# Attention's output projection of a two-layer diffusion trunk: first latents and context in one pass over the weights

## The chip, the cores and the metric

One core of a Trainium2 chip runs the whole program. The metric is the device time of one execution in microseconds (us), as the median over runs; lower is better.

## The reference

A trunk of two layers with D = 1024 works on 1024 latent tokens and 256 context tokens. Layer 0 mixes tokens by multi-head latent attention, layer 1 by bidirectional gated linear attention (GLA); each mixer is followed by an MLP with a squared ReLU. Around every mixer and MLP stand an RMS norm ahead and one behind, with shift, scale and gate per stream, and the residual sum. The part around the change, cut from the reference:

```python
y_lat = o_lat @ w_o            # latents, 1024 x 1024 by 1024 x 1024
y_ctx = o_ctx.reshape(B, C, MLA_HEADS * MLA_V) @ w_o      # context, 256 x 1024
...
def rms_norm(x, g):
    xf = x.astype(jnp.float32)
    y = xf * lax.rsqrt(jnp.mean(xf * xf, axis=-1, keepdims=True) + NORM_EPS)
    return (y * g.astype(jnp.float32)).astype(x.dtype)
def modulate(h, shift, scale):
    return h * (1.0 + scale) + shift
def sqrelu_mlp(h, w1, w2):
    return jnp.square(jax.nn.relu(h @ w1)) @ w2
```

Both streams go through the same `w_o`. Its result is normed and gated, added to x, normed and modulated again, and is then h, the operand of the MLP.

## The kernel before

Activations lie with the features on the 128 partitions (8 tiles of 128 features, index k) and the tokens along the free axis. The tokens fall into three blocks: block 0, the context (256 wide), block 1, the first latents (512), block 2, the second latents (512). A product in single precision is made of three fast ones: `split` cuts an operand into a high part (a cast on ACT, L202) and a low part (a subtraction, L199, on DVE here), and `mm3` issues three matmuls, high by high (L232), high by low (L233), low by high (L234).

The output projection runs block by block, in the order 1, 0, 2. `out_items` makes one pass: two halves of the output features; in each half four PSUM banks, one for each 128 features, add up over the eight k. For every k and half a weight tile of 128x512 (`mla_wo`) is loaded and split, so a pass loads 16 tiles. Behind each half the four banks are copied to SBUF (L808, DVE), squared (L296 or L299, ACT) and the squares added up (L300, DVE). There are eight PSUM banks in all, twelve buffers "w" for split weights (six tiles), twelve "stg" for loaded tiles, 56 "m" buffers 512 wide, 16 "c" buffers 256 wide, and four "s" buffers for rows of x.

What stands behind a block's pass is a generator, `residual_norm_steps`, put on a list `bg`. It loads four rows of x into the "s" buffers, makes the inverse root mean square (`rstd`: an all-ones matmul over the sum of squares, L307; then three ACT operations, L313 to L315; then three DVE operations, L316 to L318), scales the eight tiles (L856), adds x (L858; each add frees a buffer for one of the other four rows), stores the sum to `x_scr` (L864), adds up squares again, makes a second `rstd`, and writes h: for block 1 by a scaling on DVE (L876) and a bias on ACT (L877), for the context by L324, L326 and L327, which give the split operand at once. The loads of x keep their written order on SP.

`tick` pays steps out of that list: each weight tile of a pass gives a credit of its width x 0.005, that is 2.56 for a wide block's and 1.28 for the context's, and each yield of the generator costs a number from a table. Block 1's steps ask for 46.2 in all, the context's for 35.8. With an empty list the credit stays at zero. A pass of 16 tiles gives 41.0 for a wide block and 20.5 for the context. What is not paid out by then runs when somebody asks for it: `mlp` calls `ready(h[1])`, which runs the list until block 1's h is written, splits it, builds the first two groups of MLP products for block 1 (`up_first`, 24 wide matmuls each; each ends in a DVE add from PSUM, L885, ReLU and square on ACT, L964 and L965, and stores to `a_scr` and `hid`, L978 and L980), and only then calls `ready(h[0])`, which runs the context's steps, and builds the context's products (`up_first_ctx`). From the program so written a scheduler makes a fixed order for each engine when the kernel is built; SP issues all the transfers named here.

Of the kernel before, what the change touches and what calls it, by code (L numbers as in the profile page):

```python
# [11 lines left out]
F32R = mybir.dt.float32r  # L12
# [7 lines left out]
P = 128  # L20
D = 1024
KT = D // P
CTX = 256
# [12 lines left out]
BLK_ORDER = (1, 0, 2)  # L36
BLK = ((0, 256), (256, 512), (768, 512))
# [8 lines left out]
PLAN = {'sq': [(1, 5), (1, 7), (2, 3), (2, 7), (0, 4), (2, 4), (1, 4), (2, 1), (1, 1)],  # L46
 'xlo': [5, 7, 6, 0],
 'wlo': [7, 1, 6, 0],
# [58 lines left out]
class Trunk:  # L107
# [648 lines left out]
    def after_attention(self, stop):  # L756
        I = self.I
        self.bg, self.credit = [], 0.0
        h = {b: self.out_proj(0, b, "mla_wo", self.o_scr, 0, I["xT"]) for b in BLK_ORDER}
        self.nc.sync.dma_start(self.cl, self.c_scr)  # L760
        if stop == "wo0":
            self.drain()
            return
        h = self.mlp(0, h)
        if stop == "mlp0":
            self.drain()
            return
        h = self.gla(h)
        self.mlp(1, h)
        self.drain()  # L770
# [21 lines left out]
    def out_items(self, res, l, b, wname, src, off, xsrc):  # L792
        t0, w = BLK[b]
        acc = self.m(512)[:, :w]
        o, ys = [], []
        for half in range(2):
            pss = [self.ps(w) for _ in range(4)]
            for k in range(KT):
                if half == 0:
                    o.append(self.msplit(self.load(src[k, :, t0 - off:t0 - off + w]), w, self.nc.vector))  # L800
                ww = self.weight(self.I[wname][k * P:(k + 1) * P, half * 512:half * 512 + 512], self.nc.vector)
                for n in range(4):
                    self.mm3(pss[n], self.cols(ww, n * P), o[k], k == 0, k == KT - 1)
                self.tick(w * PLAN["tk"][0])
                yield
            for n in range(4):
                y = self.m(512)[:, :w]
                self.nc.vector.tensor_copy(y, pss[n])  # L808
                self.sumsq(acc, pss[n], half == 0 and n == 0, w)
                ys.append(y)  # L810
        self.bg.append(self.residual_norm_steps(res, l, b, ys, acc, xsrc, 2, (l, 4), (l, 3), b != 0))

    def out_half_items(self, part, acc, ys):

        c = slice(part * 256, part * 256 + 256)
        o = []
        for half in range(2):
            pss = [self.ps(256) for _ in range(4)]
            for k in range(KT):
                if half == 0 and k % 2 == 0:  # L820
                    raw = self.slot("stg", 512)
                    self.nc.sync.dma_start(raw.rearrange("p (k t) -> p k t", t=256),
                                           self.z_scr[k:k + 2, :, c].rearrange("k p t -> p k t"))
                    zs = self.msplit(raw, 512, self.nc.vector)
                    o += [self.cols(zs, 0, 256), self.cols(zs, 256, 256)]
                ww = self.weight(self.I["gla_wo"][k * P:(k + 1) * P, half * 512:half * 512 + 512], self.nc.vector)
                for n in range(4):
                    self.mm3(pss[n], self.cols(ww, n * P), o[k], k == 0, k == KT - 1)
                self.tick(PLAN["tk"][4])
                yield  # L830
            for n in range(4):
                if part == 0:
                    ys.append(self.m())
                y = ys[half * 4 + n][:, c]
                self.nc.vector.tensor_copy(y, pss[n])
                self.sumsq(acc[:, c], pss[n], half == 0 and n == 0, 256)
# [845 lines left out]
```

## Time and profile before

| | before |
|---|---|
| median of 3 runs | 2870.64 us (2866.56 to 2875.65) |
| profiled execution | 2861.42 us |
| its span, first to last instruction | 2859.6 us |
| mean granted TensorE clock | 0.984 |
| PE busy | 2736.4 us (96%) |
| DVE busy | 2283.3 us (80%) |
| ACT busy | 1594.9 us (56%) |
| DMA, mean over the span | 187 GB/s |

The three passes of the output projection lie between 698.9 and 819.7 us of the span: block 1 to 742.6, the context to 766.3, block 2 behind it. The first two groups of MLP products follow until 836.0, then the context's products. PE is the TensorE, DVE the VectorE, ACT the ScalarE, SP the engine that issues the transfers. In a row of time the bracket at the end gives how long the engine stood idle before it and which instruction ended that idle time. Matmuls overlap, so the distance between the starts of two is what one costs.

### The profile page before, as it was taken

Reading aid. Unit: us, or ns where it says so; the run is one execution under the profiler, and the core shown is the slowest. Engines: PE = TensorE matmul, PEld = TensorE weight load, DVE = VectorE, ACT = ScalarE, POOL = GpSimd, SP = SyncE. Lnnn points to the kernel's source line nnn. Section 1 sums busy time; section 2 is a strip of 40 time slices with the busy share of each in tenths; the row PEclk is TensorE's granted clock in tenths of the full one; section 3 lists DMA queues with packets and bytes.
Section 4 is the critical chain, followed back from the end, with each engine's and each line's share of the span. In section 5 each row is a group of like instructions: output and inputs, shape, how many; then the busy total and the mean of one; then the engine's idle time right before and its main releaser. Section 6 shows DMA issues by size and latency. Waiting matters only on the chain.

```text
span 2859.6 us, 44542 instructions
## 1 busy us (share of the span) xinstructions
PE 2736.4 (96%) x14774; PEld 2355.4 (82%) x14774; DVE 2283.3 (80%) x4377; ACT 1594.9 (56%) x3341; POOL 535.3 (19%) x390
## 2 busy tenths in 40 slices
PE   8999898999989999999999999999888999999998
PEld 6788787898779888888888888888787778888877
DVE  6898989987788887698868684466998999777676
ACT  4667666666566444444544456666655745555443
POOL 2554444522000000000000032565520000000000
PEclk9999999999999999999999999999899999999999
DMA  7121434323636675498735566776685667577455
GB/s 252 40 80 61 132 99 142 101 74 120 225 121 233 199 255 181 154 338 289 257 123 177 170 200 191 246 241 220 200 265 202 232 207 257 192 272 260 144 181 160
DMA packets 319528, 535.50 MB, mean 187 GB/s; under 512 B 33216, under 2 KB 96576, under 8 KB 319296
## 3 DMA queue, kind: packets, MB, share of 16 engines
q1 hardware_dynamic: 313472, 527.40, 55.8%
q10 hardware_dynamic: 5760, 5.25, 0.5%
q8 instruction: 116, 1.90, 0.3%
q14 instruction: 116, 0.95, 0.1%
q0 software_dynamic: 64, 0.00, 0.0%
HBM read 412.19 MB, written 120.32 MB: 186 GB/s over the span
## 4 chain that ended last, share of the span: by engine, by line
PE 74%; DVE 14%; DMA 4%; ACT 4%; issue 2%; POOL 1%; SPq 0%; ACTq 0%; DVEq 0%; POOLq 0%
PE ps L233 23%; PE ps L232 22%; PE ps L234 22%; DVE m L199 2%; DVE y L708 1%; PE ps L735 1%; DVE ada L251 1%; DVE w L199 1%; ACT m L202 1%; DVE m L722 1%; PE ps L703 1%; PE ps L704 1%; PE ps L705 1%; ACT m L710 1%; PE ps L707 1%
## 5 line engine op out<-in xcount | busy, mean ns | idle before, releaser
L233 PE MATMUL ps<-m,w 128*128 128x512 f32 (+1 forms) x2320 | 896.0, 388 | 14.2 <-DVE m L199 14.1
L232 PE MATMUL ps<-m,w 128*128 128x512 f32 (+1 forms) x2320 | 876.1, 388 | 19.6 <-ACT m L202 15.9
L234 PE MATMUL ps<-m,w 128*128 128x512 f32 (+1 forms) x2320 | 891.0, 387 | 0.3 <-DVE w L199 0.2
L232 PEld LDWEIGHTS ps<-m,w 128*128 128x128 f32 x2320 | 438.4, 190 | 110.7 <-ACT m L202 22.9
L233 PEld LDWEIGHTS ps<-m,w 128*128 128x128 f32 x2320 | 440.5, 190 | 105.4 <-DVE m L199 20.7
L234 PEld LDWEIGHTS ps<-m,w 128*128 128x128 f32 x2320 | 439.7, 190 | 88.8 <-DVE w L199 2.4
L202 ACT CAST w<-stg 128x512 fp32r<-128x512 f32 (+2 forms) x510 | 312.0, 616 | 309.0 <-PE ps L233 246.0
L199 DVE TENSOR_TENSOR w<-stg,w 128x512 fp32r<-128x512 f32 x412 | 297.9, 727 | 113.0 <-ACT w L202 97.7
L202 ACT CAST m<-stg 128x512 fp32r<-128x512 f32 x296 | 177.7, 625 | 138.3 <-DMA stg<-hid 121.6
L233 PE MATMUL ps<-m,m 128*128 128x256 f32 (+1 forms) x632 | 196.4, 311 | 7.6 <-DVE m L199 4.1
L199 DVE TENSOR_TENSOR m<-stg,m 128x512 fp32r<-128x512 f32 x256 | 172.0, 685 | 39.3 <-ACT m L202 38.2
L232 PE MATMUL ps<-m,m 128*128 128x256 f32 (+1 forms) x632 | 188.1, 314 | 15.0 <-DVE m L1530 8.1
L232 PE MATMUL ps<-c,w 128*128 128x256 f32 (+1 forms) x664 | 188.3, 287 | 10.8 <-ACT c L326 4.7
L234 PE MATMUL ps<-m,m 128*128 128x256 f32 (+1 forms) x632 | 192.9, 305 | 0.0
L233 PE MATMUL ps<-c,w 128*128 128x256 f32 (+1 forms) x664 | 186.4, 283 | 1.3 <-DVE c L431 1.3
L234 PE MATMUL ps<-c,w 128*128 128x256 f32 (+1 forms) x664 | 185.1, 283 | 0.0
L1296 POOL DMA_DIRECT2D m<-m x2 | 1.2, 598 | 913.8 <-PE ps L233 913.1
L199 POOL TENSOR_TENSOR w<-stg,w 128x512 fp32r<-128x512 f32 (+2 forms) x98 | 131.0, 1338 | 194.4 <-ACT w L202 155.5
L202 ACT CAST w<-m 128x512 fp32r<-128x512 f32 x128 | 79.2, 621 | 116.3 <-PE ps L233 115.9
L232 PEld LDWEIGHTS ps<-m,m 128*128 128x128 f32 x632 | 123.1, 196 | 24.4 <-DVE m L1530 8.7
L885 DVE TENSOR_TENSOR t<-ps,t 128x512 f32<-128x512 f32 x164 | 111.0, 684 | 39.4 <-PE ps L234 31.5
L964 ACT ACTIVATE t<-t 128x512 f32<-128x512 f32 x109 | 68.7, 631 | 131.2 <-DVE t L885 126.0
(300 smaller groups left out, 5878.3 us busy)
## 6 DMA issues: line engine op xcount, KB each, us to landing
stg<-in_mlp_w SPq DMA_DIRECT2D x256, 256.0 KB, 4.3
stg<-hid SPq DMA_DIRECT2D x227, 256.0 KB, 3.9
hid<-t SPq DMA_DIRECT2D x205, 256.0 KB, 3.4
stg<-in_w SPq DMA_DIRECT2D x182, 256.0 KB, 3.4
ada<-in_adaT SPq DMA_DIRECT2D x80, 512.0 KB, 3.7
stg<-in_adaT SPq DMA_DIRECT2D x112, 256.0 KB, 4.1
stg<-in_gla_wv SPq DMA_DIRECT2D x64, 256.0 KB, 3.9
stg<-in_mla_wo SPq DMA_DIRECT2D x48, 256.0 KB, 4.7
```

Source lines behind the costliest of these rows:

```text
L199: eng.tensor_tensor(out=out, in0=a, in1=bits(hi), op=ALU.subtract)
L202: self.nc.scalar.copy(hi, src)
L232: mm(ps, lhs[0], rhs[0], start=first, stop=False, skip_group_check=shared)
L233: mm(ps, lhs[0], rhs[1], start=False, stop=False, skip_group_check=shared)
L234: mm(ps, lhs[1], rhs[0], start=False, stop=last, skip_group_check=shared)
L251: pin(nc.vector.tensor_tensor_reduce(out=w, in0=w, in1=self.cs[:, s], scale=1.0, scalar=0.0, op0=ALU.mult, op1=ALU.add, accum_out=c))
L703: mm(ps, qh[:, qs], kh, start=True, stop=False)
L704: mm(ps, qh[:, qs], kl, start=False, stop=False)
L705: mm(ps, ql[:, qs], kh, start=False, stop=False)
L707: mm(ps, qr[:, qs], rl, start=False, stop=True)
L885: eng.tensor_tensor(out=out, in0=a, in1=b, op=op)
L964: self.nc.scalar.activation(c, c, AF.Relu)
```

## The change

Blocks 1 and 0 go through one pass, `out_two`: each weight tile is loaded and split once and serves 12 wide matmuls for block 1 and then 12 narrow ones for the context. Six PSUM banks add up at a time: four for block 1, and two for the context, with two groups of 256 columns in each. The context's operands lie in "m" buffers, 256 columns of them used. Block 2 keeps its pass of its own. The norm steps of blocks 1 and 0 are both put on the list behind the merged pass, block 1's first; the merged pass therefore ticks with an empty list. What follows (L849 before, L886 after, and on) is the same text, 37 lines further down; `out_items` moves by two lines.

```diff
--- before.py
+++ after.py
@@ -756,7 +756,9 @@
     def after_attention(self, stop):
         I = self.I
         self.bg, self.credit = [], 0.0
-        h = {b: self.out_proj(0, b, "mla_wo", self.o_scr, 0, I["xT"]) for b in BLK_ORDER}
+        h = {1: [], 0: []}
+        self.run(self.out_two(h))
+        h[2] = self.out_proj(0, 2, "mla_wo", self.o_scr, 0, I["xT"])
         self.nc.sync.dma_start(self.cl, self.c_scr)
         if stop == "wo0":
             self.drain()
@@ -809,6 +811,41 @@
                 self.sumsq(acc, pss[n], half == 0 and n == 0, w)
                 ys.append(y)
         self.bg.append(self.residual_norm_steps(res, l, b, ys, acc, xsrc, 2, (l, 4), (l, 3), b != 0))
+
+    def out_two(self, h):
+
+        V = self.nc.vector
+        acc = {b: self.m(512)[:, :BLK[b][1]] for b in (1, 0)}
+        o, ys = {1: [], 0: []}, {1: [], 0: []}
+        for half in range(2):
+            pss = [self.ps() for _ in range(4)]
+            psc = [self.ps() for _ in range(2)]
+            for k in range(KT):
+                if half == 0:
+                    for b in (1, 0):
+                        t0, w = BLK[b]
+                        hi, lo = self.slot("m", w, F32R), self.slot("m", w, F32R)
+                        self.split(self.load(self.o_scr[k, :, t0:t0 + w]), hi, lo, V)
+                        o[b].append((hi, lo))
+                ww = self.weight(self.I["mla_wo"][k * P:(k + 1) * P, half * 512:half * 512 + 512], V)
+                for n in range(4):
+                    self.mm3(pss[n], self.cols(ww, n * P), o[1][k], k == 0, k == KT - 1)
+                for n in range(4):
+
+                    self.mm3(psc[n // 2][:, (n % 2) * CTX:(n % 2) * CTX + CTX], self.cols(ww, n * P), o[0][k],
+                             k == 0 and n % 2 == 0, k == KT - 1, True)
+                self.tick(768 * PLAN["tk"][0])
+                yield
+            for b in (1, 0):
+                w = BLK[b][1]
+                for n in range(4):
+                    p = pss[n] if b else psc[n // 2][:, (n % 2) * CTX:(n % 2) * CTX + CTX]
+                    y = self.m(512)[:, :w]
+                    V.tensor_copy(y, p)
+                    self.sumsq(acc[b], p, half == 0 and n == 0, w)
+                    ys[b].append(y)
+        for b in (1, 0):
+            self.bg.append(self.residual_norm_steps(h[b], 0, b, ys[b], acc[b], self.I["xT"], 2, (0, 4), (0, 3), b != 0))
 
     def out_half_items(self, part, acc, ys):
```

Of transfers there are 2022 on SP before and 2006 after: 16 loads of weight tiles fewer. The number of matmuls is the same. Where steps move, engine by engine:

On SP, before, the context's last four loads of x and its first stores stand while block 2's pass runs (`in_w` are MLP weights, `in_xT` the rows of x, `x_scr` the residual sum):

```order
L212 DMA stg_10498<-in_w 128x512
L212 DMA s_9805<-in_xT 128x256
L864 DMA x_scr<-m_9184 128x256
L212 DMA s_9811<-in_xT 128x256
L864 DMA x_scr<-m_9187 128x256
L212 DMA s_9837<-in_xT 128x256
L864 DMA x_scr<-m_9192 128x256
L212 DMA s_9845<-in_xT 128x256
```

After, all eight loads of the context's x stand behind the stores of the first two groups of MLP products (L1015 and L1017 are L978 and L980 before, L901 is L864):

```order
L212 DMA stg_10466<-in_w 128x512
L212 DMA stg_10472<-in_w 128x512
L1015 DMA a_scr<-t_9786 128x512
L1015 DMA a_scr<-t_9832 128x512
L1017 DMA hid_97<-t_9787 128x512
L1017 DMA hid_97<-t_9833 128x512
L212 DMA s_9866<-in_xT 128x256
L212 DMA s_9868<-in_xT 128x256
L212 DMA s_9870<-in_xT 128x256
L212 DMA s_9872<-in_xT 128x256
L212 DMA s_9886<-in_xT 128x256
```

The context's loads thus moved behind four stores that wait for the results of the MLP's first products.

On PE, the two all-ones matmuls of the context's norm before (`ps_9661` is an accumulator of block 2's pass, `ps_10020` one of the MLP products, `ps_10095` the context's first MLP product):

```order
L234 MATMUL ps_9664<-m_9504,w_9742 128x512
L307 MATMUL ps_9757<-m_8970,ones 128x256
L232 MATMUL ps_9661<-m_9537,w_9768 128x512
...
L234 MATMUL ps_10020<-m_9942,w_10001 128x512
L307 MATMUL ps_10038<-m_9802,ones 128x256
L232 MATMUL ps_10095<-c_10049,w_9948 128x256
```

And after (`ps_9848` and `ps_9802` belong to the MLP products, `ps_9995` is the context's first MLP product):

```order
L232 MATMUL ps_9848<-m_9749,w_9828 128x512
L307 MATMUL ps_9874<-m_8588,ones 128x256
L233 MATMUL ps_9802<-m_9750,w_9782 128x512
...
L234 MATMUL ps_9848<-m_9770,w_9829 128x512
L307 MATMUL ps_9938<-m_9883,ones 128x256
L232 MATMUL ps_9995<-c_9949,w_9776 128x256
```

The first of the two moved from inside block 2's pass to inside the 48 MLP matmuls, 26 of which stand ahead of it; the second still stands directly ahead of the context's products. Block 1's second all-ones matmul moved as well: 48 matmuls of block 2's pass stood ahead of it before, 168 stand ahead of it now.

On DVE, before, the low parts of block 1's h (L199 from an "m" into an "m" buffer), operands of the MLP products, stand among the last adds of the context's x (L858) and of its squares (L300):

```order
L858 TENSOR_TENSOR m_9409<-m_9409,s_9837 128x256
L199 TENSOR_TENSOR m_9915<-m_9583,m_9914 128x512
L199 TENSOR_TENSOR m_9919<-m_9610,m_9918 128x512
L858 TENSOR_TENSOR m_9414<-m_9414,s_9845 128x256
L199 TENSOR_TENSOR m_9923<-m_9613,m_9922 128x512
L199 TENSOR_TENSOR m_9927<-m_9640,m_9926 128x512
L300 TENSOR_TENSOR m_9802<-m_9802,t_9848 128x256
L199 TENSOR_TENSOR m_9931<-m_9683,m_9930 128x512
```

After, the last of these low parts stand around the context's first norm (L316 to L318) and behind its eight scalings (L893 is L856 before, L913 is L876):

```order
L199 TENSOR_TENSOR m_9757<-m_9753,m_9756 128x512
L913 SCALAR_TENSOR_TENSOR m_9760<-m_9223,m_78,m_9618 128x512
L316 SCALAR_TENSOR_TENSOR m_8588<-m_8588,c_9876 128x256
L317 TENSOR_TENSOR m_8588<-m_8588,c_9876 128x256
L318 SCALAR_TENSOR_TENSOR c_9876<-m_8588,c_9876 128x256
...
L199 TENSOR_TENSOR m_9764<-m_9760,m_9763 128x512
L913 SCALAR_TENSOR_TENSOR m_9767<-m_9228,m_78,m_9618 128x512
L893 SCALAR_TENSOR_TENSOR m_8949<-m_8949,m_80,c_9876 128x256
...
L893 SCALAR_TENSOR_TENSOR m_9248<-m_9248,m_80,c_9876 128x256
L199 TENSOR_TENSOR m_9771<-m_9767,m_9770 128x512
L922 TENSOR_TENSOR t_9787<-ps_9802,t_9786 128x512
```

The last low part is thus made after the context's scalings, directly ahead of the adds that end the MLP products (L922, before L885).

## Rows read from the trace of the kernel before

**Rows 1.** The page: the chain that ended last, by engine.

```profile
PE 74%; DVE 14%; DMA 4%; ACT 4%; issue 2%; POOL 1%; SPq 0%; ACTq 0%; DVEq 0%; POOLq 0%
```

**Rows 2.** By stretch: us, each engine's busy us, PEclk, DMA share, GB/s.

```profile
698.90:742.40 43.50, 43.50 (x192) 36.00 (x193) 26.88 (x47) 21.36 (x40) 0.00 (x0) 1.00 0.79 267
...
766.30:776.90 10.60, 4.32 (x13) 3.07 (x13) 10.60 (x21) 5.49 (x11) 0.00 (x0) 0.68 0.83 278
...
819.60:836.60 17.00, 13.81 (x51) 10.36 (x50) 14.27 (x29) 10.53 (x21) 0.00 (x0) 0.90 0.47 149
...
841.30:1000.00 158.70, 158.70 (x871) 137.96 (x872) 140.95 (x242) 92.09 (x172) 0.00 (x0) 0.99 0.61 199
```

**Rows 3.** Groups by line, 698.9 to 766.3: busy us, mean ns, idle before.

```profile
L202 ACT CAST w<-stg 128x512 fp32r<-128x512 f32 x37 | 23.0, 621 | 20.4 <-PE ps L233 16.8 <-DMA stg<-in_mla_wo 2.9 <-ACT t L299 0.3
...
L199 DVE TENSOR_TENSOR w<-stg,w 128x512 fp32r<-128x512 f32 x33 | 22.6, 687 | 14.1 <-ACT w L202 9.6 <-PE ps L233 2.2 <-DMA stg<-in_mla_wo 2.0
```

**Rows 4.** PE in time, two block borders: start us, us, what, idle before.

```profile
742.37 0.39 PE L234 MATMUL ps<-m,w 128*128 128x512 f32 x1
742.60 0.28 PE L232 MATMUL ps<-c,w 128*128 128x256 f32 x1
742.71 0.28 PE L233 MATMUL ps<-c,w 128*128 128x256 f32 x1
...
768.90 1.27 PE L232 MATMUL ps<-m,w 128*128 128x512 f32 x4 [2.58 <-ACT m L202]
...
773.88 0.80 PE L233 MATMUL ps<-m,w 128*128 128x512 f32 x1 [3.70 <-DVE m L199]
...
774.90 0.63 PE L233 MATMUL ps<-m,w 128*128 128x512 f32 x1
775.32 0.63 PE L234 MATMUL ps<-m,w 128*128 128x512 f32 x1
```

**Rows 5.** PE in time: all-ones matmuls (L307) and waits behind block 2's pass.

```profile
785.55 0.67 PE L307 MATMUL ps<-m,ones 128*128 128x512 f32 x1
...
808.30 0.38 PE L307 MATMUL ps<-m,ones 128*128 128x256 f32 x1
...
820.81 0.50 PE L232 MATMUL ps<-m,w 128*128 128x512 f32 x1 [1.00 <-ACT m L202]
823.50 0.73 PE L232 MATMUL ps<-m,w 128*128 128x512 f32 x2 [2.19 <-ACT m L202]
...
836.03 0.60 PE L307 MATMUL ps<-m,ones 128*128 128x256 f32 x2
841.28 0.59 PE L232 MATMUL ps<-c,w 128*128 128x256 f32 x2 [4.65 <-ACT c L326]
```

**Rows 6.** DVE and ACT in time: durations of wide and narrow operations.

```profile
741.11 1.88 DVE L808 COPY m<-ps 128x512 f32<-128x512 f32 x3
...
789.18 0.68 DVE L316 SCALAR_TENSOR_TENSOR m<-m,m 128x512 f32<-128x512 f32 x1
...
813.17 3.26 DVE L856 SCALAR_TENSOR_TENSOR m<-m,m,c 128x256 f32<-128x256 f32 x8
...
837.03 0.62 ACT L964 ACTIVATE t<-t 128x512 f32<-128x512 f32 x1
...
838.81 0.42 DVE L316 SCALAR_TENSOR_TENSOR m<-m,c 128x256 f32<-128x256 f32 x1 [1.82 <-ACT c L315]
```

**Rows 7.** SP's queue in time: the context's x loads and their stores.

```profile
816.79 0.33 SPq L212 DMA_DIRECT2D s<-in_xT  x1
817.17 0.42 SPq L864 DMA_DIRECT2D x_scr<-m  x1
817.69 0.38 SPq L212 DMA_DIRECT2D s<-in_xT  x1
```

**Rows 8.** DMA issues, 810 to 830 us; landing of x loads, 780 to 830.

```profile
s<-in_xT SPq DMA_DIRECT2D x4, 128.0 KB, 2.7
...
DMA to landing us min/median/max: 2.1/2.9/4.5
```

## The prediction

> **What bounds the kernel now.** I read the chain that ended last first: PE holds 74% of it, DVE 14% [rows 1]. So a saving on another engine is worth something only where PE waits for it, and I looked for PE's waits in the stretch that the change rewrites. The table by stretch shows them [rows 2]. Block 1's pass, 698.9 to 742.4, has PE busy all through. At the start of block 2's pass PE works 4.32 of 10.60 us at a granted clock of 0.68, while DVE is busy for all 10.60. At 819.6 to 836.6, the first MLP products, it works 13.81 of 17.0; from 836.6 to 841.28 it stands still for the context's norm, with a wait of 4.65 [rows 5]. From 841.3 to 1000 it is busy for 158.70 of 158.70: behind 841.3 nothing can swallow a delay for a long way. The whole case is therefore one question: when does the context's first MLP matmul start, today 841.28?
>
> **The removed work is hidden.** The change drops 16 weight loads, 16 ACT casts and 16 DVE subtractions of 128x512. In the two passes that are merged, the cast costs 0.62 us and the subtraction 0.69, but both engines' idle time ahead of them ends with PE: 16.8 of the casts' 20.4 us of idle time, that is, they wait for PE to give back weight buffers [rows 3]. 16 x 0.62 = 9.9 us of ACT and 16 x 0.69 = 11.0 us of DVE lie beside PE's busy 43.5 us, and are worth nothing there. The number of matmuls does not change: a wide one follows the next at 0.23 us, a narrow one at 0.12 [rows 4], so the merged pass is 192 x 0.227 + 192 x 0.119 = 66.4 us of PE in either order. Its start may slip by 0.3 us, since two operands are split ahead of the second weight tile. The merged pass then ends at 698.9 + 0.3 + 66.4 = 765.6, with block 1's last matmul 12 narrow ones before, at 764.2 instead of 742.6.
>
> **Step 1, block 2's start: a gain.** Before, PE ran 11 matmuls there in the 10.6 us from 766.3 to 776.9, worth 11 x 0.227 = 2.5: 8.1 us lost, to two waits (2.58 and 3.70) and to the low clock behind them, 1.2 instead of 2.4 GHz (0.43 us a matmul in place of 0.23) [rows 2, 4]. DVE caused it, busy with block 1's first norm. After, that norm has not begun, but another wait comes: the all-ones matmul for block 1's sums stands 4 matmuls into block 2, at about 766.5, and the sums need four wide copies (0.63), three narrow ones (as a narrow scaling, 0.41), three wide adds (taken as copies) and a weight subtraction on DVE: 4 x 0.63 + 3 x 0.41 + 3 x 0.63 + 0.69 = 6.3 [rows 3, 6]. The first copies run while the last accumulators fill, 1.4 us ahead of 764.2; I take 764.2 + 5.1 = 769.3 for the sums. PE waits 2.9 us and loses 1 to 1.7 us to the clock: about 4 lost for 8.1, **a gain of 4**. Block 2 ends at 765.6 + 43.6 + 4.5 + 1.1 for its two all-ones matmuls = 814.8, against 819.6 now.
>
> **Step 2, block 1's second norm: the gain is lost.** The steps of the norms are paid out by ticks: 20.5 us from block 0's pass and 41 from block 2's before, 41 alone after, since the list is empty during the merged pass. Block 1 asks for 46.2. Its second all-ones matmul, at 785.55 now [rows 5], moves to 168 matmuls into block 2, about 808.5. From there its chain reaches DVE after 3.6 us (785.55 to 789.18) [rows 5, 6], at 812.1; four operations of 0.6 (three for the norm, one weight subtraction), four scalings of 0.68, block 2's four copies, a weight subtraction and the operand's own subtraction make 812.1 + 2.4 + 2.7 + 2.4 + 0.6 + 0.1 = 820.3 for the first operand of the MLP. PE waits 5.3 us at its start, where it now waits 1.00 and 2.19 [rows 5]. The last operand comes later still, because DVE's order puts the context's first norm ahead of it: three small operations and eight scalings (3.26 us for the eight). That norm's all-ones matmul stands 26 matmuls into the 48 of the MLP, at 828 in place of 808.30; its chain reaches DVE after 2.8 us (836.03 to 838.81), and 1.3 for the three operations, 0.6 and 0.7 for an operand between, 3.3 for the scalings and 0.6 for the last subtraction [rows 5, 6] bring the last operand at 837.2, and the 48 matmuls end at **837.7, where they end at 836.03 now**.
>
> **Step 3, the context's norm: the loss.** Today the context's eight rows of x are loaded and added inside block 2's pass and behind it: from 816.79 on they run on SP as load, store, load, store, a pair each 0.95 us [rows 7], and only the second all-ones matmul and its chain (836.03 to 841.28, 5.25 us) are left at the end of the MLP products [rows 5, 7]. After, SP's order has the four stores of the MLP's results ahead of these loads; SP works in order, so the loads go out when the second result is there. From 837.7: the DVE adds of both results to 839.1 (2 x 0.69), two wide ACT passes of 0.62 [rows 6] and the store: the first load at about 841.0, the fourth at 842.1. A load of 128 KB lands 2.7 us after issue (median of four; of seven loads around it the least 2.1 and the most 4.5) [rows 8]. The first add frees its buffer at 844.1, and the other four loads leave at 0.95 us a pair, the last at 847.0; it lands at 849.7, and add, square and add make 850.9. Then the chain of 5.25 us: **the context's matmul at 856.1 against 841.28, +14.8 us.** What is queued behind the waiting stores on SP (the eight loads, the stores of x, the next MLP weights) has one impatient reader, this norm. PE stands still from 837.7 to 856 but for the all-ones matmul, about 18 us for 4.65 now.
>
> The operands of the context lie in wider buffers (the 56-deep pool instead of the 16-deep one). The rows show no wait on either; I price that from 0 to +1 us and take 0. From 841.3 on PE has no idle time to give back [rows 2], so the 14.8 us stay.
>
> **The rivals.** (A) **Covered after all, faster.** In the place of step 3, SP could reach the loads early. If the first results of the MLP came out some 20 us sooner than I order them, the norm would again run under PE's products; then step 1's 4 us remain and the stall at 836 (4.65) goes: -8.7, 2861.9. It decides at a first load before about 824. Against it speaks that these stores depend on PE's last matmul, and that PE's own start waits for DVE. (B) **Half the price, same.** The loads of the second four are not held back by buffers, and land in 2.1 us; the norm is then bound by DVE alone: sixteen operations of 0.41 us, 6.6 us from 840. All-ones at about 842.5, context at 847.5: +6, within what can be told from no change only just. For it: with the loads of the MLP's weights held back, DMA is quiet there, and 2.1 has been seen [rows 8]; against: there are four buffers for eight loads. (C) **The order as I add it**, +14.8. (D) **The spare banks run out.** Six accumulators leave two banks free for the next group, four before. At the merged pass's middle and at its end PE must wait for a copy (0.63) and a square ahead of each further accumulator, and each accumulator is 3 x 0.227 = 0.68 us of PE: a small wait if DVE does nothing else, 0.69 for each weight subtraction in between, up to five: 3.4 us a boundary and 6.9 for both, on top of C: +22. The Trainium skill (Perfetto Trace Analysis, Matmul Optimizations) wants all 8 PSUM banks used so that independent work overlaps, and its section on matmuls there wants groups to rotate through banks so that evacuation runs under the next group; this change holds six in one group, so by that rule D would be the case. Here the row on DVE's copies (0.63, below the 0.68 of an accumulator) speaks against most of it. That the change does not do what it says is excluded by the order of the engines: SP has 16 instructions fewer, all loads of this weight.
>
> **How the numbers follow.** The profiled run took 2861.42 us, 9.2 below the median of 2870.64, and the runs spread over 9.1; I add the shift to the median. C: 2870.64 + 14.8 = 2885.4. A difference of about 0.3% (8.6 us) is what a measurement can tell from no change. Chances: C 0.65, D 0.13, B 0.16, A 0.06. A is faster; B gives 2876.6, the same; C and D (2893) are slower, but C with landings of 2.1 in both batches (-1.2), a median at the low end (-4) and a late norm cheaper by 2 would be 2878, so a little of it (0.03) is the same. Faster 0.06, same 0.19, slower 0.75. The range takes B's upper part and D: C with landings of 4.5 us in both batches is +3.6, with D +10.5; I take 2874 to 2896.
>
> **What would show it.** Right: PE idle for 15 to 19 us ahead of the context's first matmul at 853 to 859, with the context's first load issued only behind the second result's store; PE at block 2's start waiting once, about 3 us, for the sums; the MLP's 48 matmuls ending within 2 us of 836. Step 1 is wrong if block 2's pass ends later than 819.6; step 2 if its all-ones matmul comes before 800; step 3 if the context's loads are issued before 835. A PE wait for a DVE copy in the middle of the merged pass would be D. And the whole is wrong if idle time of PE behind 1000 shrinks by as much as it grew here.

## The result, and the profile after

The changed kernel takes **2897.77 us** (2897.67 to 2901.66, 4 runs) against 2868.6 (2865.0 to 2875.65, 4 runs): ratio 1.0103, interval 1.0089 to 1.0117. It is slower by 29.2 us, where 14.8 were forecast; the range ended at 2896.

The span by stretch, as in [rows 2], cut at the borders that the changed program has: the merged pass; block 2's start; the rest of its pass; the 48 MLP matmuls; the context's norm; the context's products; block 2's norm.

```profile
700.90:769.40 68.50, 68.50 (x384) 60.20 (x384) 30.72 (x55) 24.13 (x45) 0.00 (x0) 0.98 0.51 177
769.40:780.80 11.40, 7.15 (x19) 4.85 (x18) 7.79 (x18) 6.56 (x14) 0.00 (x0) 0.70 0.21 70
780.80:822.10 41.30, 41.30 (x181) 33.51 (x179) 35.15 (x58) 19.48 (x35) 0.00 (x0) 1.00 0.61 204
822.10:845.90 23.80, 15.39 (x51) 10.22 (x50) 20.31 (x37) 14.54 (x27) 0.00 (x0) 0.90 0.13 44
845.90:864.00 18.10, 1.22 (x3) 0.50 (x2) 8.70 (x22) 7.24 (x17) 0.00 (x0) 0.50 0.45 145
864.00:889.60 25.60, 25.57 (x170) 23.37 (x170) 23.44 (x45) 14.22 (x29) 0.00 (x0) 0.92 0.44 143
889.60:900.00 10.40, 2.38 (x5) 1.20 (x5) 8.58 (x16) 5.84 (x12) 0.00 (x0) 0.62 1.02 354
```

The second number is PE's busy time. It is full in the merged pass and in block 2's pass behind its start, and PE stands nearly still in two stretches: one of 18.1 us ahead of the context's products, which the prediction named, and one of 10.4 us behind them, which it did not. PE's own rows, which answer to [rows 4] and [rows 5]:

```profile
700.88 0.72 PE L232 MATMUL ps<-m,w 128*128 128x512 f32 x1 [2.59 <-ACT w L202]
...
773.86 2.08 PE L232 MATMUL ps<-m,w 128*128 128x512 f32 x4 [4.25 <-ACT m L202]
775.73 1.91 PE L307 MATMUL ps<-m,ones 128*128 128x512 f32 x2
...
815.63 1.02 PE L307 MATMUL ps<-m,ones 128*128 128x512 f32 x2
824.35 0.50 PE L232 MATMUL ps<-m,w 128*128 128x512 f32 x1 [2.23 <-ACT m L202]
...
835.57 0.60 PE L307 MATMUL ps<-m,ones 128*128 128x256 f32 x2
...
858.91 1.22 PE L307 MATMUL ps<-m,ones 128*128 128x256 f32 x2 [13.01 <-DVE m L300]
864.02 0.80 PE L232 MATMUL ps<-c,w 128*128 128x256 f32 x2 [3.90 <-ACT c L326]
...
897.67 2.07 PE L307 MATMUL ps<-m,ones 128*128 128x512 f32 x2 [8.02 <-DVE m L300]
```

The 13.01 us are the wait of step 3. SP's queue (compare [rows 7]) and DVE show its parts:

```profile
847.91 0.84 SPq L1017 DMA_DIRECT2D hid<-t  x2
848.80 3.29 SPq L212 DMA_DIRECT2D s<-in_xT  x5
852.14 0.43 SPq L901 DMA_DIRECT2D x_scr<-m  x1
852.68 0.36 SPq L212 DMA_DIRECT2D s<-in_xT  x1
```

```profile
846.01 0.69 DVE L922 TENSOR_TENSOR t<-ps,t 128x512 f32<-128x512 f32 x1 [0.23 <-PE ps L234]
851.31 0.79 DVE L895 TENSOR_TENSOR m<-m,s 128x256 f32<-128x256 f32 x2 [4.61 <-DMA s<-in_xT]
852.77 0.76 DVE L895 TENSOR_TENSOR m<-m,s 128x256 f32<-128x256 f32 x2 [0.67 <-DMA s<-in_xT]
```

The first load of the context's x goes out at 848.80, right behind the store of the second MLP result, and DVE waits 4.61 us for it. The wait in the row at 897.67 is new. It is the second all-ones matmul of **block 2's** norm, which had no wait before:

```profile
877.71 1.02 PE L307 MATMUL ps<-m,ones 128*128 128x512 f32 x2
```

In PE's order before the change, 48 wide and 190 narrow matmuls stand between this norm's two all-ones matmuls; after it 24 wide and 142 narrow. 24 x 0.227 + 48 x 0.119 = 11.2 us of PE work went behind it, and DVE's sums are not there so soon: from the first to the second it took 36.05 us before and 33.05 now, 8.02 of these waiting.

To compare kernels without what happens elsewhere, the tables below use one length from the traces: from the start of PE's 4001st matmul, ahead of the first pass, to the 9774th from the end, behind block 2's norm (all the kernels have 14774 matmuls). It is 202.1 us before and 234.5 after, **+32.4**. What lies ahead of it and behind it, up to PE's last matmul, is edited in no kernel and still varies by some us (692.9 to 699.8 and 1949.7 to 1957.2 us in the fourteen traces; one kernel that was traced twice has 693.3 and 697.9 ahead, 1952.3 and 1956.4 behind). So the single profiled executions lie 40 us apart, and the medians 29. The trace of the kernel before is itself a short one, 7 to 12 us below that kernel's medians: every kernel here differs from it by 2 to 7 us more in this length than in the medians. Differences among the other traces are the safer ones.

### The profile page after: what moved, and what is told of

Read it like the earlier page. It is cut to its first block, busy times and chain, and to the rows that moved or that the text cites. A ratio compares the mean times of both kernels' runs of the same rounds, so it can differ in the third digit from the quotient of the medians.

```text
span 2899.9 us, 44447 instructions
## 1 busy us (share of the span) xinstructions
PE 2749.5 (95%) x14774; PEld 2363.9 (82%) x14774; DVE 2273.2 (78%) x4361; ACT 1589.8 (55%) x3325; POOL 531.8 (18%) x390
## 3 DMA queue, kind: packets, MB, share of 16 engines
q10 hardware_dynamic: 5760, 5.25, 0.5%
## 4 chain that ended last, share of the span: by engine, by line
PE 73%; DVE 14%; DMA 5%; ACT 4%; issue 3%; POOL 1%; SPq 0%; DVEq 0%; ACTq 0%; POOLq 0%
PE ps L232 22%; PE ps L233 22%; PE ps L234 22%; DVE m L199 2%; PE ps L735 1%; DMA stg<-hid 1%; DVE y L708 1%; DVE ada L251 1%; DVE w L199 1%; ACT m L202 1%; PE ps L703 1%; PE ps L307 1%; PE ps L704 1%; PE ps L705 1%; PE ps L706 1%
## 5 line engine op out<-in xcount | busy, mean ns | idle before, releaser
L233 PE MATMUL ps<-m,w 128*128 128x512 f32 (+1 forms) x2384 | 917.2, 386 | 14.6 <-DVE m L199 14.5
L232 PE MATMUL ps<-m,w 128*128 128x512 f32 (+1 forms) x2384 | 901.0, 387 | 21.7 <-ACT m L202 16.5
L234 PE MATMUL ps<-m,w 128*128 128x512 f32 (+1 forms) x2384 | 906.1, 384 | 2.9 <-DVE w L199 2.9
L232 PEld LDWEIGHTS ps<-m,w 128*128 128x128 f32 x2384 | 452.0, 190 | 115.0 <-ACT m L202 24.5
L233 PEld LDWEIGHTS ps<-m,w 128*128 128x128 f32 x2384 | 453.6, 190 | 106.3 <-DVE m L199 20.3
L234 PEld LDWEIGHTS ps<-m,w 128*128 128x128 f32 x2384 | 451.6, 190 | 92.1 <-DVE w L199 4.9
L202 ACT CAST w<-stg 128x512 fp32r<-128x512 f32 (+2 forms) x494 | 301.7, 615 | 357.5 <-PE ps L233 284.6
L199 DVE TENSOR_TENSOR w<-stg,w 128x512 fp32r<-128x512 f32 x396 | 286.5, 727 | 139.9 <-ACT w L202 126.4
L202 ACT CAST m<-stg 128x512 fp32r<-128x512 f32 (+1 forms) x304 | 180.4, 619 | 145.6 <-DMA stg<-hid 124.8
L199 DVE TENSOR_TENSOR m<-stg,m 128x512 fp32r<-128x512 f32 (+1 forms) x264 | 175.7, 681 | 54.0 <-ACT m L202 53.1
L232 PE MATMUL ps<-c,w 128*128 128x256 f32 (+1 forms) x600 | 170.2, 288 | 10.0 <-ACT c L326 3.9
L233 PE MATMUL ps<-c,w 128*128 128x256 f32 (+1 forms) x600 | 168.3, 283 | 1.3 <-DVE c L431 1.3
L199 POOL TENSOR_TENSOR w<-stg,w 128x512 fp32r<-128x512 f32 (+2 forms) x98 | 131.8, 1345 | 196.8 <-ACT w L202 153.3
L234 PE MATMUL ps<-c,w 128*128 128x256 f32 (+1 forms) x600 | 166.8, 283 | 0.0
L922 DVE TENSOR_TENSOR t<-ps,t 128x512 f32<-128x512 f32 x164 | 111.1, 684 | 41.0 <-PE ps L234 34.8
L199 DVE TENSOR_TENSOR w<-m,w 128x512 fp32r<-128x512 f32 x128 | 87.3, 686 | 65.8 <-ACT w L202 56.4
```

The source lines that it names most:

```text
L199: eng.tensor_tensor(out=out, in0=a, in1=bits(hi), op=ALU.subtract)
L202: self.nc.scalar.copy(hi, src)
L232: mm(ps, lhs[0], rhs[0], start=first, stop=False, skip_group_check=shared)
L233: mm(ps, lhs[0], rhs[1], start=False, stop=False, skip_group_check=shared)
L234: mm(ps, lhs[1], rhs[0], start=False, stop=last, skip_group_check=shared)
L922: eng.tensor_tensor(out=out, in0=a, in1=b, op=op)
```

## The experiments

**More ticks for block 2's pass.** The merged pass ticks with an empty list, so only 41.0 of the 61.4 remain. This gives them back:

```diff
-                self.tick(w * PLAN["tk"][0])
+                self.tick(w * PLAN["tk"][0] * (1.5 if (l, b) == (0, 2) else 1))
```

> The changed kernel, with 1.5 times the ticks in block 2's pass (61.4 in 16 tiles, what blocks 0 and 2 gave together before). The order then has block 1's second all-ones matmul 92 matmuls behind its first, the context's first one inside block 2's pass again, and block 2's second one 238 matmuls behind its first, as before the change. Theory T (the lost ticks cost the time): the 13.0 us and 8.0 us waits for the sums of squares go, only the later start of block 2's pass stays (about +5 in the traces): 2872 to 2878 us, about 20 to 25 below the changed kernel. Rival M (the merging itself costs it: six banks, eight accumulators to empty at block 2's start): at most 8 below the changed kernel, 2890 or more.

Measured: 2876.12 us (8 runs) against 2870.88, ratio 1.0026 (1.001 to 1.0042); the length is 214.4. Both waits for sums are gone; PE's waits from 690 to 910 us (in total, times, longest) are for operands, nearly all for casts:

```profile
PE ps L232 <- ACT m L202: 14.4, 5, 5.6
PE ps L232 <- ACT c L326: 5.6, 1, 5.6
PE ps L232 <- ACT w L202: 2.6, 1, 2.6
PE ps L233 <- POOL m L199: 1.3, 2, 1.0
```

So 20.1 of the 32.4 us, and 24 of the 29 in the medians, come from the ticks. The weights are shared here just as in the changed kernel. What stays, 12.3 us in the trace, is more than the 5 that I expected: counted from the first pass's first matmul, 1.3 us of it are there at the end of the merged pass, and 8.3 behind block 2's start, where PE waits 4.26 and 5.57 us for casts (2.58, and 3.70 for a subtraction, before).

**The kernel before with fewer ticks.** The opposite edit: two passes, nothing merged, and no ticks in block 0's pass.

```diff
-                self.tick(w * PLAN["tk"][0])
+                if (l, b) != (0, 0):
+                    self.tick(w * PLAN["tk"][0])
```

> The kernel before, two passes as they were, only without the ticks in block 0's pass: block 1's norm then starts with block 2's pass and the context's norm behind the first MLP products, as in the changed kernel. Theory T: slower by nearly the whole of the change's cost, 18 to 28 us, 2887 to 2897; at block 2's start it may win back up to 8.1 us since block 1's norm is no longer there. Rival M: within 4 us of the kernel before.

Measured: 2892.18 us (4 runs) against 2870.88, ratio 1.0083 (1.0061 to 1.0104); length 229.1, +27.0. PE waits at the same two places as in the changed kernel, and as long:

```profile
850.59 1.22 PE L307 MATMUL ps<-m,ones 128*128 128x256 f32 x2 [13.42 <-DVE m L300]
...
890.49 2.07 PE L307 MATMUL ps<-m,ones 128*128 128x512 f32 x2 [8.41 <-DVE m L300]
```

Most of the slowdown thus needs no merging. The two experiments together show that the change is slow, for the larger part, because of which norm steps run during which pass. Of the 5.4 us between this trace and the changed kernel's, 1.0 lies ahead of the first pass and 1.6 is a low clock at its start, which isn't the change's (last section).

**The context's x early.** In the changed kernel, the eight loads are issued ahead of the MLP's first products; the norm's steps stay.

```diff
         h[2] = self.out_proj(0, 2, "mla_wo", self.o_scr, 0, I["xT"])
+        self.cx = [self.load(I["xT"][k, :, :CTX], "c") for k in range(KT)]
...
-        xs = [self.load(xsrc[k, :, t0:t0 + w], "s") for k in range(4)]
+        xs = self.cx if (l, b, gate) == (0, 0, 2) else [self.load(xsrc[k, :, t0:t0 + w], "s") for k in range(4)]
...
```

> The changed kernel, with the context's eight rows of x loaded ahead of the MLP's first products into 256-wide buffers that the merged pass left free; its norm steps stay where they are. If the place of the loads on SP is what the context waits for (step 3 of the prediction): the wait of 13.0 us ahead of the context's second all-ones matmul falls to 3 to 6, and the time by 7 to 10, to 2888 to 2891. If DVE would have been late anyway: the wait stays above 9 and the time falls by less than 4. The wait of 8.0 us ahead of block 2's second all-ones matmul stays in either case.

Measured: 2892.44 us (4 runs), ratio 1.0084 (1.0058 to 1.011); length 227.4, 7.1 less than the changed kernel.

```profile
855.39 1.22 PE L307 MATMUL ps<-m,ones 128*128 128x256 f32 x2 [4.36 <-DVE m L300]
```

The wait is 4.36 instead of 13.01: 8.65 us of it were the place of the loads on SP. A part comes back ahead of it, where a PE wait for the last operand of the MLP grew from 1.63 to 2.63, since DVE now makes three of the context's adds ahead of that operand. The median fell by 5.3, less than the 7 to 10 that I expected. The changed kernel was measured in another series, though; against the medians of the kernel before in each series (2868.6 and 2870.88) the gain is 7.6.

**One number of the table.** Block 2's second inverse root mean square costs 18 instead of 8 ticks, in the changed kernel:

```diff
- 'yield': [[[3.0, 6.0, 1.3, 8.0, 8.4, 1.3], [3.0, 8.4, 1.3, 8.0, 6.0, 1.3], [3.0, 6.0, 1.3, 8.0, 6.0, 1.3],
+ 'yield': [[[3.0, 6.0, 1.3, 8.0, 8.4, 1.3], [3.0, 8.4, 1.3, 8.0, 6.0, 1.3], [3.0, 6.0, 1.3, 18.0, 6.0, 1.3],
```

> The changed kernel with one number of the table changed (the price ahead of block 2's second inverse root mean square 18 instead of 8): block 2's second all-ones matmul stands 238 matmuls behind its first, as before the change, instead of 166; nothing else moves up to there. If that place is what PE's wait of 8.0 us and the low clock behind it come from: faster by 8 to 11 us, 2887 to 2890. Rival (PE would then wait for the same sums later, at block 2's operands): faster by less than 3 us.

Measured: 2886.98 us (6 runs), ratio 1.0058 (1.0037 to 1.0079), 10.8 below the changed kernel (13.1 against the medians before); length 224.1, 10.4 less.

```profile
903.62 1.02 PE L307 MATMUL ps<-m,ones 128*128 128x512 f32 x2
```

No wait is left at this matmul and none took its place: the 8.02 us and the low clock behind it came from its place in the order alone.

**Block 2's first operands early.** In the changed kernel, two of block 2's operands are loaded and split within the merged pass's last two weight tiles.

```diff
+                if half == 1 and k == KT - 2:
+                    self.pre = [self.msplit(self.load(self.o_scr[i, :, 768:1280]), 512, V) for i in range(2)]
                 ww = self.weight(self.I["mla_wo"][k * P:(k + 1) * P, half * 512:half * 512 + 512], V)
...
```

In `out_items`, block 2 then takes these two in place of loads of its own.

> The changed kernel, with block 2's first two operands loaded and split within the merged pass's last two weight tiles, ahead of the copies and squares that empty its six banks. If PE's wait of 4.25 us at block 2's start comes from ACT's casts standing behind those squares: the wait falls to under 1.5, the low clock behind it goes too, and the time falls by 4 to 7, to 2891 to 2894. If the evacuation itself holds PE (a bank not yet free): the wait stays above 3 under another name and the time moves by less than 2.

Measured: 2893.34 us (4 runs), ratio 1.0092 (1.007 to 1.0114), 4.4 below the changed kernel; length 231.4, 3.1 less.

```profile
771.95 1.02 PE L307 MATMUL ps<-m,ones 128*128 128x512 f32 x2
...
774.92 1.18 PE L232 MATMUL ps<-m,w 128*128 128x512 f32 x4 [1.95 <-ACT m L202]
...
776.80 0.63 PE L234 MATMUL ps<-m,w 128*128 128x512 f32 x1
777.23 0.63 PE L233 MATMUL ps<-m,w 128*128 128x512 f32 x1
```

The wait of 4.25 is gone; 1.95 is left for the third operand, more than the 1.5 that I expected. The low level didn't go: behind this wait eight matmuls start 0.43 us apart. Counted from the first pass's first matmul, block 2's pass ends 3.4 us earlier. 0.9 of this is lost again at the MLP's start, where more matmuls run at the low level; the two waits for sums hardly move (12.87 and 8.37 us).

**The three edits together**, with the ticks left as the change has them:

> The changed kernel with three single edits together: block 2's first two operands split early, the context's x loaded early, block 2's second all-ones matmul back at 238. The ticks stay as the change left them. From the pass's start to behind block 2's norm the three gave 3.1, 7.1 and 10.4 us by themselves (stretch of 234.5 us against 202.1 before). If they are separate waits in series: stretch 234.5 - 20.6 = 213.9, median 2876 to 2880. If they share a cause further down (DVE late with the same sums): the stretch stays above 218.

Measured: 2876.86 us (12 runs) against 2873.02, ratio 1.0014 (1.0003 to 1.0026); length 212.8 for 213.9 expected. The three waits stand in series, and what the edits give adds up.

**The operands of block 2 all ahead.** With the ticks given back, all eight operands of block 2 split in the merged pass's second half. The context's operands lie in the 256-wide "c" buffers here, so two edits stand beside the ticks:

```diff
+                if half == 1 and k < 8:
+                    self.pre.append(self.msplit(self.load(self.o_scr[k, :, 768:1280]), 512, V))
                 ww = self.weight(self.I["mla_wo"][k * P:(k + 1) * P, half * 512:half * 512 + 512], V)
...
```

> The changed kernel with 1.5 times the ticks in block 2's pass (as in the first experiment), the context's operands in 256-wide buffers, and all eight operands of block 2 loaded and split within the merged pass's second half. Theory T: of what stays over before in the first experiment (+12 in the trace up to block 2's norm, +5 in the medians) the waits of 4.26 and 5.57 us for the casts of block 2's operands go, with the low clock behind them: 8 to 12 below that experiment, 2862 to 2868, faster than before by 3 to 9. Rival: DVE is late with the norms whatever stands ahead, and the time stays at 2874 to 2878.

Measured: 2874.14 us (10 runs) against 2868.3, ratio 1.0022 (1.0009 to 1.0035); length 209.7. A miss: the waits for casts at block 2's start went, and a wait of the kind removed elsewhere came.

```profile
798.38 2.07 PE L307 MATMUL ps<-m,ones 128*128 128x512 f32 x2 [9.37 <-DVE m L300]
```

This is block 1's second all-ones matmul: PE, without its earlier stalls, comes to it 14.2 us behind the first one (774.81), before DVE has the sums, and can start it only at 23.6. The kernel before has 124 narrow matmuls of block 0's pass between them.

The same operands split ahead in the kernel before, without merging:

```diff
+                if half == 1 and (l, b) == (0, 0):
+                    self.pre.append(self.msplit(self.load(self.o_scr[k, :, 768:1280]), 512, self.nc.vector))
                 ww = self.weight(self.I[wname][k * P:(k + 1) * P, half * 512:half * 512 + 512], self.nc.vector)
...
```

> The kernel before, two passes as they were, with all eight operands of block 2 loaded and split within the second half of block 0's pass. It tells whether the gain of the last kernel needs the merged pass. Before, PE lost 8.1 us at block 2's start to casts and subtractions of operands behind block 1's norm. If these go: 5 to 8 us below the kernel before, 2863 to 2866, and the merging is worth 0 to 3 beside it. Rival: block 0's pass, with 20.4 of 23.9 us of DVE busy, can't take eight more subtractions (5.5 us), and the wait only moves: within 3 us of before.

Measured: 2863.84 us (10 runs) against 2868.3, ratio 0.9985 (0.9972 to 0.9997): 4.5 below, a little less than the 5 to 8 expected. It was measured once more:

> The two-pass kernel with block 2's operands split ahead, the same text as before in its experiment, to see whether its ratio of 0.9985 stands: its trace has 203.6 us for the stretch where the kernel before has 202.1, so by the trace it is no faster: ratio 0.999 to 1.002. If the first measurement was right: 0.997 to 0.9995.

2868.77 us (12 runs) against 2873.02, ratio 0.9986 (0.9971 to 1.0). It is the fastest kernel of this study, below both, by an amount at the edge of what can be measured. Its length in the two traces is 203.6 and 204.3, not less than the 202.1 before. 2.0 and 2.3 us more than before pass up to the end of block 1's pass, which the edit doesn't touch, mostly at a low clock; behind it the two are 0.5 and 0.1 ahead. Where the 4 us of the medians lie isn't shown.

**Weight subtractions on GpSimd.** Block 2's 16, in the last merged kernel, in the last two-pass kernel, and in the kernel before.

```diff
-                ww = self.weight(self.I[wname][k * P:(k + 1) * P, half * 512:half * 512 + 512], self.nc.vector)
+                ww = self.weight(self.I[wname][k * P:(k + 1) * P, half * 512:half * 512 + 512],
+                                 self.nc.gpsimd if (l, b) == (0, 2) else self.nc.vector)
```

> The merged kernel with 1.5 times the ticks and block 2's operands split ahead, and the sixteen weight subtractions of block 2's pass on GpSimd, which is idle there, in place of VectorE. PE waited 9.4 us in that kernel for block 1's second sum of squares on DVE. If DVE's load is what makes these sums late (16 x 0.60 us of slots go from its queue within block 2's pass), the wait falls to under 4 and the time by 5 to 9 below that kernel, to 2865 to 2870. Rival: GpSimd's subtraction takes 1.34 us, slows DVE beside it or comes late for PE: no gain, 2874 or more.

> The two-pass kernel with block 2's operands split ahead, and the weight subtractions of block 2's pass on GpSimd. If DVE's load sets PE's waits at the borders of block 2's pass (1.52, 1.96, 1.31, 2.54 and 5.05 us in that kernel): 3 to 7 below it, 2857 to 2861, and the best of all. If the waits are chains rather than load: within 2 us of it.

> The kernel before with one edit, the weight subtractions of block 2's pass on GpSimd. DVE is busy for all 10.60 us at block 2's start, where PE loses 8.1: if load alone is the cause, 4 to 8 below before, 2860 to 2865; if the place of the operands' casts and subtractions in the queues is the cause, within 3 us of before.

Measured: 2872.65 (1.0008, 0.9997 to 1.0018), 2871.86 (1.0007, 0.9995 to 1.0019) and 2871.85 us (1.0011, 0.9998 to 1.0024) against 2870.0: no gain clear of noise in any. In the merged kernel the wait for block 1's second sums grew, from 9.37 to 11.66 us, where I expected under 4. The lengths of the two-pass kernels grew, from 203.6 to 207.5 and from 202.1 to 206.9; 2.3 of the last 4.8 us lie ahead of the end of block 1's pass and are not the edit's. The kernel before with this edit shows where the rest comes from. DVE's eight block 1 scalings before:

```profile
761.09 5.38 DVE L856 SCALAR_TENSOR_TENSOR m<-m,m,m 128x512 f32<-128x512 f32 x8
```

The same eight while GpSimd subtracts, GpSimd's row, and the last two of the eight by themselves:

```profile
763.13 11.54 DVE L857 SCALAR_TENSOR_TENSOR m<-m,m,m 128x512 f32<-128x512 f32 x8
```

```profile
762.50 10.29 POOL L199 TENSOR_TENSOR w<-stg,w 128x512 fp32r<-128x512 f32 x6 [69.38 <-ACT w L202]
```

```profile
773.26 1.40 DVE L857 SCALAR_TENSOR_TENSOR m<-m,m,m 128x512 f32<-128x512 f32 x2
```

They start 0.66 us apart before. Here each of the first six takes 1.67 to 1.71 us until the next one starts; the last two, behind GpSimd's last subtraction (it ends at 772.8), stand 0.66 apart again. PE waits 7.53 us behind them. The work that left DVE's queue slowed what stayed in it.

## Why the prediction was right and wrong

The length from the pass's start to behind block 2's norm, in one table:

| kernel | length, us | against before |
|---|---|---|
| before | 202.1 | |
| changed | 234.5 | +32.4 |
| before, fewer ticks | 229.1 | +27.0 |
| changed, ticks given back | 214.4 | +12.3 |
| changed, x early | 227.4 | +25.3 |
| changed, block 2's norm later | 224.1 | +22.0 |
| changed, operands early | 231.4 | +29.3 |
| changed, the three together | 212.8 | +10.7 |

**The direction and the mechanism held, but for a third of the cost.** The removed weights are worth nothing on PE, and 21.7 of the 32.4 us are there at the context's first MLP matmul, because the ticks moved its norm behind the first MLP products. Both tick experiments show it from either side. Two steps failed: step 1, whose gain did not come, and the sentence that the 14.8 us stay, which missed a second late norm.

**Steps 2 and 3 held, in size too.** Block 1's second all-ones matmul was put 6.3 us ahead of block 2's end (808.5 to 814.8) and stands 6.5 ahead (815.63 to 822.1). The MLP's 48 matmuls were put at 22.9 us and took 23.8. From their end to the context's matmul 18.4 us were worked out and 18.1 measured, part by part: first load 3.3 us behind the end and 2.9 measured, the sums 13.2 and 13.0, the chain 5.25 and 5.1. The loads landed in 2.7 us, the number taken from [rows 8].

**Step 1 failed.** It gave a gain of 4, and was to be wrong if block 2's pass ended later than 819.6; it ended at 822.1. The merged pass took 68.6 us from its first matmul instead of 66.4, the larger part since PE's first eight matmuls ran at the low clock (0.43 us each); it also began 0.7 later than the shift of what lies ahead and the 0.3 allowed explain. At block 2's start the sums were not what PE waited for. ACT had two narrow squares, each waiting for a copy on DVE, ahead of the casts of block 2's operands, and PE waited 4.25 us for these. I had counted DVE's queue there and not ACT's:

```profile
772.52 0.78 ACT L299 ACTIVATE t<-ps 128x256 f32<-128x256 f32 x2 [1.56 <-DVE m L844]
773.19 1.13 ACT L202 CAST m<-stg 128x512 fp32r<-128x512 f32 x2
```

Block 2's pass with its start took 52.65 us for 53.4 before: a gain of 0.7, not 4. Start, pass and block 2 make 0.7 + 2.2 + 3.5 = 6.4 us of the miss, the MLP 0.9, step 3 takes 0.3 back: 7.0, so the context's matmul came 21.7 us late instead of 14.8. Splitting those operands early removed the 4.25, which shows that part. The low clock at the pass's start is not the merged order's (last section), so about 2 of the 2.9 us of start and pass go with that clock and not with the change.

**The sentence that the 14.8 us "stay" was wrong.** It rested on PE being busy for 158.70 of 158.70 us behind 841.3 in the kernel before [rows 2], and took the order behind the context's products as given. The order had moved there too: with the credit spent otherwise, block 2's second all-ones matmul stood 72 matmuls earlier, and the shift grew from 22.7 to 33.4. These 10.7 us are not in the sum at all. 14.8 + 6.9 + 10.7 = 32.4: the 33.4 less the 1.0 by which the whole stretch began later in this trace. The number that gave this back (10.4 in the trace, 10.8 in the medians) was one entry of a table.

**The rivals.** D, the spare banks, did not happen: PE is busy for 68.50 of 68.50 us over the merged pass with its middle, so six accumulators cost no wait there that the profile shows. In the merged kernel with GpSimd's subtractions, whose pass ran at the high level, its 383rd matmul starts 66.4 us behind its first, where the sum gave 66.4 for all 384. The wait that by the prediction would follow from the Trainium skill's rule on using all eight banks (Perfetto Trace Analysis, Matmul Optimizations) thus doesn't show within the pass. At its end eight accumulators are emptied with no narrow pass to cover it, and part of the 12.3 us that stay when the ticks are given back lies there: PE's wait at block 2's start was 4.26 us in that kernel too. A and B did not happen: the first load of x left at 848.80, behind the store, and the loads of the second four waited for their buffers. B's price was also added wrongly: sixteen operations of 0.41 us from 840 end at 846.6 and not at 842.5, and the chain of 5.25 us then gives +10.6, not +6.

## What to carry to other kernels

When a pass that paid out background work disappears, its share of that work goes with it. Count what each pass pays and what each list asks before and after, and then look up the new place of **every** consumer of that work, up to the last one in the list, not only of the first that is late. For each moved wait, go through the queues of all the engines that feed it, ACT's and SP's as well as DVE's. And run the inverse edit: taking the ticks from the old kernel gave 27.0 of the 32.4 us without the change itself.

## What the hardware showed that I had not expected

DVE's scaling of 128x512 went from 0.66 to about 1.70 us each while GpSimd subtracted 128x512 tiles beside it, and GpSimd's subtraction from 1.28 us, with DVE idle (789.88 to 793.60 in the same trace), to 1.71 and more: the two went on in step. The Trainium skill (Perfetto Trace Analysis, Optimizing Scalar/DVE Operations) says that the two share a read port of SBUF, so that moving work between them might not help; the traces agree here, with these numbers. DVE was not slowed by GpSimd everywhere. Beside a row of DVE's additions one subtraction of GpSimd lasted 6.74 us, by a profile that is rough for this engine, and the wide additions kept their 0.60 us:

```profile
783.18 6.74 POOL L199 TENSOR_TENSOR w<-stg,w 128x512 fp32r<-128x512 f32 x1 [10.39 <-ACT w L202]
```

The clock at the first pass's start did not follow the length of the wait. Behind 2.29 us of waiting the kernel before ran its first four matmuls in 1.21 us, the high level; the two-pass kernel with block 2's operands split ahead had the same wait and took 2.02 us for the same four, the low level:

```profile
698.90 1.21 PE L232 MATMUL ps<-m,w 128*128 128x512 f32 x4 [2.29 <-ACT w L202]
```

```profile
697.59 2.02 PE L232 MATMUL ps<-m,w 128*128 128x512 f32 x4 [2.29 <-ACT w L202]
```

Neither level belongs to one order. The kernel before with GpSimd's subtractions, the same program up to there, waited 2.29 us as well and began at the low level: block 1's pass took 45.3 us up to the next one's first matmul, and 43.7 in the kernel before. The merged kernel with these subtractions began at the high level, behind the 2.59 us of waiting that the changed kernel has. The first eight matmuls of the two, with the granted clock as the last number but two:

```profile
700.90:704.30 3.40, 3.40 (x8) 2.73 (x9) 3.28 (x7) 2.20 (x5) 0.00 (x0) 0.51 0.87 260
```

```profile
700.30:702.10 1.80, 1.80 (x8) 1.48 (x9) 1.80 (x5) 1.47 (x4) 0.00 (x0) 1.00 0.78 221
```

The first is the changed kernel. What decides between the levels is open; some 1.6 of the merged pass's 68.6 us are of this kind and not the change's.
